# First feed-forward block, larger token group: the input projection by seven block products in halves of 192 tokens

## The chip, the cores and the metric

The kernel runs on one core of one Trainium2 chip. The metric is the device time of one execution in microseconds. Before the change it is 1551.35 us, the median of three runs (1550.58 to 1552.38).

## The reference, cut to what matters

The reference runs one step of a streaming encoder: a convolution layer with a SwiGLU feed-forward block, then a shared key and value projection, an attention layer and a second feed-forward block, for 640 tokens (512 of a prompt, 128 of eight running streams). All of it is in 32-bit floats. The change touches the first feed-forward block:

```python
D_MODEL = 1024
FFN_HIDDEN = -(-8 * D_MODEL // (3 * 256)) * 256        # 2816

def rms_norm(x, g):
    xf = x.astype(jnp.float32)
    y = xf * lax.rsqrt(jnp.mean(xf * xf, axis=-1, keepdims=True) + EPS)
    return (y * g.astype(jnp.float32)).astype(x.dtype)

def swiglu_ffn(h, g, w_in, w_out):
    a, b = jnp.split(rms_norm(h, g) @ w_in, 2, axis=-1)
    return h + (jax.nn.silu(a) * b) @ w_out
```

With 128 rows to a tile, `w_in` has 8 blocks in depth and 22 hidden tiles, each with an `a` half and a `b` half of 128 columns; `w_out` has 22 blocks in depth and 8 output tiles.

## The kernel before

Activations lie with their features on the 128 partitions and the tokens along the row. The residual stream `h` stays on the chip. The tokens are split into a smaller group 0 of 256 and a larger group 1 of 384 tokens (`GR`).

Every 32-bit product is made of three matmuls. A weight tile is loaded as `raw`, rounded by ScalarE to `whi` (fp32r), and the rest `wlo = raw - whi` is formed by VectorE, or by VectorE and GpSimd, which take the share that `pool` names in quarters (`wsplit`, L150 and L154). Activations are split in the same way (`xsplit`, L159 and L160). `mm3` (L170, L171, L172) then adds whi by xhi, wlo by xhi and whi by xlo into one PSUM bank. Each matmul has its own load of a 128x128 weight.

A hidden tile of the feed-forward block is made by `ffn_in`: one weight load of 128x2048 (both halves, 1 MB), two chains of 24 matmuls for each token group, and behind them the gate. `rms_late` leaves the per-token scale out of the activations, so the gate multiplies both halves by it (`bc`, L290 to L293) where the group has such a scale. The hidden tiles of a chunk (4 or 6 of them) are kept, and `ffn_out` multiplies them with the chunk's blocks of `w_out`, adding each output tile to `h` (L303).

The hidden tiles are dealt out as follows. Group 0 does tiles 0 to 17 in three chunks (`FS`) while the convolution of group 1 still runs on VectorE. Then `pw2` of group 1 completes its `h` (L506), and `rms_late` of group 1 (the step "r1" of `PLAN`) makes its activations. Both groups do tiles 18 to 21 together, with each weight split used for both (`FC`). Group 1 then does tiles 0 to 17 alone (`FD`).

The second feed-forward block already makes its input projection in another way, for halves of 320 tokens (`Unit`, L968 in `prod`): the four blocks of the weight (two halves of depth, by `a` and `b`) and the four blocks of the activations (two halves of depth, by two halves of the tokens) are combined by additions so that seven block products, `m1` to `m7`, stand for eight. Some of the additions are made on the weights (L913, VectorE and GpSimd), some on the activations once, and some on the results in PSUM.

The order of instructions on each engine is set by a scheduler that goes by dependencies and by the priorities given in `tc.high_priority`. All weight loads go through one queue (SyncE), into two buffers of `raw`, `whi` and `wlo` each (`wp`). Four PSUM banks (`mm`) and two pairs of banks (`w2`) serve this part.

Of the kernel before, what the change touches and what calls it, by code (L numbers as in the profile page):

```python
# [8 lines left out]
F32 = mybir.dt.float32  # L9
# [33 lines left out]
FD = ((0, 6), (6, 6), (12, 6))  # L43
# [26 lines left out]
PLAN = ("a0 y a1 a2 a4 x a3 a5 a6 l04 p04 l05 d0213 a7 b0 p05 b1 l07 p07 l06 b2 q00 s0 p06 n0 b3 b4 b5 d145 l13 w0 b7 r0 p13 b6 f q16 s1 d101 d127 n1 f f w1 r1")  # L70
# [7 lines left out]
def tile_trunk(ctx, tc, xT, vecs, hist, w_pw1, w_pw2, w_in0, w_out0, w_in1, w_out1,  # L78
# [13 lines left out]
    def nm(s):  # L92
        uid[0] += 1
        return f"{s}_{uid[0]}"
# [176 lines left out]
    def ffn_in(wsrc, j, xs, hid, jj, groups, pool):  # L271
        wh, wl = wsplit(wsrc[j], 16, P, pool=pool)
        for g in groups:
            n = GR[g][1]
            ps = []
            for ab in range(2):
                pt = mmt()
                mm3(pt[:, :n], [(wh[:, (ab * 8 + k) * P:(ab * 8 + k + 1) * P],
                                 wl[:, (ab * 8 + k) * P:(ab * 8 + k + 1) * P]) for k in range(KT)],
                    xk(xs[g], range(KT)))  # L280
                ps.append(pt[:, :n])
# [39 lines left out]
    def ffn(pool, w_in, w_out, xs, groups, chunks, pl=0, og=None, cm=CM, pad=(0, 0)):  # L321
        for j0, ch in chunks:
# [8 lines left out]
            ffn_out(w_out, j0, ch, hid, og or groups, pl)  # L331

# [222 lines left out]
    xs0, xs1 = late[0], late[1]  # L555
# [3 lines left out]
    ffn({0: hp0}, w_in0, w_out0, {0: xs0}, (0,), chunks, PFB)  # L559
# [6 lines left out]
    xs = [rms_late(0, None), rms_late(1, None)]  # L566
# [324 lines left out]
    ENG = {"v": nc.vector, "p": nc.gpsimd}  # L891
    B11, B21, B22, T1, T2, T3, T4 = range(7)
# [18 lines left out]

    def add(e, out, a, b, op=ALU.add):
        ENG[e].tensor_tensor(out=out, in0=a, in1=b, op=op)  # L913

    def copy(out, src):
        nc.scalar.activation(out=out, in_=src, func=AF.Copy)
# [44 lines left out]

    def prod(ps, w, x, first):
        wh, wl = w
        xh, xl = x
        for k in range(4):
            c = slice(k * P, (k + 1) * P)
            for i, (a, b) in enumerate(((wh, xh), (wl, xh), (wh, xl))):
                nc.tensor.matmul(ps, a[:, c], b[:, k, :], start=(first and k == 0 and i == 0),  # L968
                                 stop=(k == 3 and i == 2), skip_group_check=not first)

    def quarter(hi, lo, i):
        return hi[:, 512 * i:512 * i + 512], lo[:, 512 * i:512 * i + 512]

    class Unit:
        def __init__(u, j, hid, jj):
            u.j, u.hid, u.jj = j, hid, jj

        def prep(u, a22=None):
            r = wp.tile([P, 2048], F32, tag="raw", name=nm("raw"))
            nc.sync.dma_start(r, w_in1[u.j])  # L980
            hi = wp.tile([P, 2048], F32R, tag="whi", name=nm("whi"))
            lo = wp.tile([P, 2048], F32R, tag="wlo", name=nm("wlo"))
            if a22 is None:
                bk = wf.tile([P, 2 * 1536], F32R, tag="bk", name=nm("bk"))
                a22 = bk[:, 0:512], bk[:, 1536:2048]
            else:
                bk = None
            q = u.q = [r[:, 512 * i:512 * i + 512] for i in range(4)]
            u.r = r[:, 0:1024]
            with tc.high_priority(offset=HP):  # L990
                xsplit(r[:, 0:1024], hi[:, 0:1024], lo[:, 0:1024])
                xsplit(q[2], *a22)
                add(WE[0], q[0], q[0], q[3], ALU.subtract)
                add(WE[1], q[3], q[3], q[2])
                add(WE[2], q[2], q[2], q[0], ALU.subtract)
                xsplit(r[:, 1024:2048], hi[:, 1024:2048], lo[:, 1024:2048])
                add(WE[3], q[1], q[1], q[2], ALU.subtract)
            u.a11, u.a12, u.s2, u.s1 = [quarter(hi, lo, i) for i in range(4)]
            u.a22 = a22
            if bk is not None:  # L1000
                u.prep_back(bk)

        def prep_back(u, bk=None):
            if bk is None:
                bk = wf.tile([P, 2 * 1536], F32R, tag="bk", name=nm("bk"))
            bh, bl = bk[:, 512:1536], bk[:, 2048:3072]
            with tc.high_priority(offset=HP):
                xsplit(u.r, bh, bl)
            u.s3, u.s4 = [quarter(bh, bl, i) for i in range(2)]

        def m1(u):
            u.pa = bank("pa")[:, 0:HT]
            u.u = tmp("acc")
            prod(u.pa, u.a11, xc[B11], True)
            with tc.high_priority(offset=2 * HP):
                copy(u.u, u.pa)

        def m5(u):
            u.pc = bank("pc")[:, 0:HT]
            u.v = tmp("sq")  # L1020
            prod(u.pc, u.s1, xc[T1], True)
            with tc.high_priority(offset=2 * HP):
                copy(u.v, u.pc)

        def m6(u):
            u.pb = bank("pb")[:, 0:HT]
            prod(u.pb, u.s2, xc[T2], True)
            with tc.high_priority(offset=2 * HP):
                add("v", u.pb, u.pb, u.u)
                add("v", u.pc, u.pb, u.v)  # L1030
# [241 lines left out]
```

## Time and profile before

| what | value |
|---|---|
| median of three runs | 1551.35 us |
| the profiled execution | 1551.3 us |
| its span | 1549.5 us |
| shared tiles 18 to 21 of both groups | about 422 to 506 us of the span |
| group 1 alone, tiles 0 to 17 | about 506 to 732 us |
| second feed-forward block's entry | about 1080 to 1200 us |

In the page, PE is TensorE's matmuls and PEld its weight loads, DVE is VectorE, ACT is ScalarE, POOL is GpSimd. A row of the span in slices gives the busy share in tenths. Matmuls overlap each other, so the length of one says less than the distance from one start to the next; the end of a matmul is modelled. In the order of time, the first column is the start in us from the span's start and the second the length.

### The profile page before, as it was taken

What the parts mean: (1) busy time and instruction counts of PE and PEld (TensorE: products, weight loads), DVE (VectorE), ACT (ScalarE), POOL (GpSimd) and SP (SyncE); (2) the same over time, 40 slices, a digit from 0 to 9 for tenths busy, and PEclk for the clock granted to TensorE, in tenths of its full rate; (3) what the DMA queues carried; (4) which work ended last, traced back from release to release, by engine and by line L of the source; (5) the groups of instructions that cost most, each with busy time, mean ns of one, the idle gap of its engine ahead of it and who ended that gap; (6) DMA issues with size and microseconds to landing.
All of it is one profiled execution on the core that took longest, in us unless ns stands there. A gap on an engine that the chain in (4) does not pass through costs nothing.

```text
span 1549.5 us, 26569 instructions
## 1 busy us (share of the span) xinstructions
PE 1471.7 (95%) x10770; PEld 1398.9 (90%) x10770; DVE 1050.1 (68%) x1863; ACT 662.4 (43%) x1173; POOL 443.8 (29%) x403
## 2 busy tenths in 40 slices
PE   5888998989999999999999999999989999999997
PEld 5878888989999999999988798886989999999997
DVE  6994999988555455457576767566796476476455
ACT  4544454535423323235454445443554244244244
POOL 6865568877501000001321211110411121121110
PEclk9999999999999999999999999998999999999998
DMA  7784434444421333433655545453103213213211
GB/s 236 234 228 142 137 113 159 148 157 153 147 82 55 129 116 129 135 118 126 202 183 201 174 140 205 133 175 114 55 28 109 82 56 109 82 55 109 82 55 68
DMA packets 59658, 199.95 MB, mean 129 GB/s; under 512 B 10128, under 2 KB 22672, under 8 KB 46736
## 3 DMA queue, kind: packets, MB, share of 16 engines
q1 hardware_dynamic: 59248, 197.96, 39.1%
q8 instruction: 84, 1.38, 0.4%
q10 hardware_dynamic: 288, 0.31, 0.1%
q14 instruction: 38, 0.31, 0.1%
HBM read 187.02 MB, written 11.22 MB: 128 GB/s over the span
## 4 chain that ended last, share of the span: by engine, by line
PE 71%; DVE 16%; ACT 3%; issue 3%; DMA 3%; POOL 2%; SPq 0%; POOLq 0%; DVEq 0%; ACTq 0%
PE mm L170 12%; PE mm L172 12%; PE mm L171 12%; PE pb L968 6%; DVE w L437 5%; DVE wlo L154 4%; PE pc L968 4%; PE pa L968 4%; PE pb L170 1%; PE pb L171 1%; PE pb L172 1%; PE pa L172 1%; PE pa L170 1%; PE pc L170 1%; PE pc L172 1%
## 5 line engine op out<-in xcount | busy, mean ns | idle before, releaser
L171 PE MATMUL mm<-x,wlo 128*128 128x256 f32 (+1 forms) x1344 | 416.8, 312 | 15.4 <-DVE wlo L154 14.9
L170 PE MATMUL mm<-x,whi 128*128 128x256 f32 (+1 forms) x1344 | 413.3, 312 | 6.4 <-ACT x L159 3.7
L172 PE MATMUL mm<-x,whi 128*128 128x256 f32 (+1 forms) x1344 | 412.7, 311 | 0.5
L150 ACT ACTIVATE whi<-raw 128x2048 fp32r<-128x2048 f32 (+2 forms) x117 | 197.7, 1694 | 232.6 <-PE mm L172 138.8
L171 PEld LDWEIGHTS mm<-x,wlo 128*128 128x128 f32 x1344 | 257.1, 192 | 18.7 <-DVE wlo L154 17.5
L170 PEld LDWEIGHTS mm<-x,whi 128*128 128x128 f32 x1344 | 254.5, 191 | 11.2 <-ACT x L159 4.1
L172 PEld LDWEIGHTS mm<-x,whi 128*128 128x128 f32 x1344 | 255.1, 191 | 2.9 <-DVE x L160 1.8
L154 DVE TENSOR_TENSOR wlo<-raw,whi 128x2048 fp32r<-128x2048 f32 (+5 forms) x117 | 214.0, 1832 | 62.2 <-ACT whi L150 61.2
L154 POOL TENSOR_TENSOR wlo<-raw,whi 128x1536 fp32r<-128x1536 f32 (+3 forms) x50 | 145.7, 2918 | 69.0 <-ACT whi L150 69.0
L913 POOL TENSOR_TENSOR raw<-raw 128x512 f32<-128x512 f32 x38 | 50.5, 1330 | 332.3 <-DVE raw L913 257.5
L171 PE MATMUL mm<-hid,wlo 128*128 128x256 f32 (+1 forms) x352 | 107.7, 308 | 6.6 <-DVE wlo L154 6.6
L172 PE MATMUL mm<-hid,whi 128*128 128x256 f32 (+1 forms) x352 | 105.8, 307 | 0.2
L170 PE MATMUL mm<-hid,whi 128*128 128x256 f32 (+1 forms) x352 | 104.6, 307 | 0.1
L437 DVE SCALAR_TENSOR_TENSOR w<-gp,dwv,w 128x384 f32<-128x384 f32 x180 | 103.9, 612 | 0.8
L195 POOL TENSOR_TENSOR acc<-sq,sq 128x384 f32<-128x384 f32 (+1 forms) x8 | 8.1, 1006 | 258.2 <-ACT sq L179 258.1
L171 PEld LDWEIGHTS mm<-hid,wlo 128*128 128x128 f32 x352 | 66.0, 188 | 7.8 <-DVE wlo L154 7.8
L417 POOL TENSOR_TENSOR y<-y,cvt 128x256 f32<-128x256 f32 (+1 forms) x60 | 69.3, 1154 | 6.3 <-ACT cvt L416 4.0
L172 PEld LDWEIGHTS mm<-hid,whi 128*128 128x128 f32 x352 | 65.7, 188 | 0.6 <-DVE hid L160 0.6
L159 ACT ACTIVATE whi<-raw 128x1024 fp32r<-128x1024 f32 x38 | 39.4, 1054 | 61.6 <-PE pc L172 18.1
L170 PEld LDWEIGHTS mm<-hid,whi 128*128 128x128 f32 x352 | 65.2, 188 | 0.4 <-ACT hid L159 0.3
L968 PE MATMUL pa<-x0f,whi 128*128 128x320 f32 x228 | 61.2, 316 | 2.5 <-DVE t L913 2.3
L195 POOL TENSOR_TENSOR acc<-acc,sq 128x384 f32<-128x384 f32 (+1 forms) x48 | 52.7, 1097 | 28.9 <-ACT sq L179 27.5
(317 smaller groups left out, 3391.4 us busy)
## 6 DMA issues: line engine op xcount, KB each, us to landing
raw<-in_w_in SPq DMA_DIRECT2D x62, 1024.0 KB
raw<-in_w_out SPq DMA_DIRECT2D x36, 768.0 KB
raw<-in_w_pw SPq DMA_DIRECT2D x22, 1024.0 KB
cache<-in_ck SPq DMA_DIRECT2D x32, 512.0 KB
cache<-in_cv SPq DMA_DIRECT2D x32, 512.0 KB
raw<-in_w_kq SPq DMA_DIRECT2D x8, 1024.0 KB
x<-sc SPq DMA_DIRECT2D x16, 368.0 KB
raw<-in_w_out SPq DMA_DIRECT2D x4, 1024.0 KB
```

The costliest lines, as they stand in the source:

```text
L150: nc.scalar.activation(out=hi[:, a:b], in_=raw[:, a:b], func=AF.Copy)
L154: eng.tensor_tensor(out=lo[:, a:b], in0=raw[:, a:b], in1=hi[:, a:b].bitcast(F32), op=ALU.subtract)
L159: nc.scalar.activation(out=hi, in_=src, func=AF.Copy)
L170: nc.tensor.matmul(ps, wh, xh, start=(i == 0), stop=False)
L171: nc.tensor.matmul(ps, wl, xh, start=False, stop=False)
L172: nc.tensor.matmul(ps, wh, xl, start=False, stop=(i == last))
L195: last["acc"] = eng.tensor_tensor(out=acc[:, :n], in0=prev, in1=s(), op=ALU.add)
L417: nc.gpsimd.tensor_tensor(out=y[g][:, c, :], in0=y[g][:, c, :], in1=pr[:, :n], op=ALU.add)
L437: nc.vector.scalar_tensor_tensor(out=dst, in0=src, scalar=wj, in1=dst, op0=ALU.mult, op1=ALU.add)
L913: ENG[e].tensor_tensor(out=out, in0=a, in1=b, op=op)
L968: nc.tensor.matmul(ps, a[:, c], b[:, k, :], start=(first and k == 0 and i == 0), stop=(k == 3 and i == 2), skip_group_check=not first)
```

## The change

The larger group's part of the first feed-forward block now uses the seven block products too, for all its 22 hidden tiles, in halves of 192 tokens. The code of `Unit` and its helpers moves up and takes a description of the stage (`First` or `Second`: where weights, PSUM, temporaries and results lie).

- `FC` (tiles 18 to 21) runs for group 0 alone, with three quarters of the low part of each weight on GpSimd (`PFB`).
- "r1" leaves the plan. In its place group 1's `h` is scaled by the gain on ScalarE, the row scale is formed as before, and the scaled activations are combined into seven operands of 4 x 192 columns, each split into hi and lo.
- `FD` becomes chunks of 5, 6, 5 and 6 tiles, each tile one `Unit`: `prep` loads 1 MB and makes seven split weight operands of 512 columns, `m1` to `m7` are 12 matmuls of 192 columns each, and PSUM results are added on VectorE between them.
- The eight output tiles of a chunk are dealt out between the units of the next one (`outs1`), each with its own load of `w_out`.
- The host stores the `b` half's two depth halves in swapped order; `ffn_in` reads them so.

```diff
-FD = ((0, 6), (6, 6), (12, 6))
+FD = ((0, 5), (5, 6), (11, 5), (16, 6))
+HQ = 192
+TQ = (slice(0, HQ), slice(HQ, 2 * HQ))
...
-PLAN = ("... n1 f f w1 r1")
+PLAN = ("... n1 f f w1")
...
+    def prod(ps, w, x, first):
+        wh, wl = w
+        xh, xl = x
+        for k in range(4):
+            c = slice(k * P, (k + 1) * P)
+            for i, (a, b) in enumerate(((wh, xh), (wl, xh), (wh, xl))):
+                nc.tensor.matmul(ps, a[:, c], b[:, k, :], start=(first and k == 0 and i == 0),
+                                 stop=(k == 3 and i == 2), skip_group_check=not first)
...
+            with tc.high_priority(offset=HP):
+                xsplit(r[:, 0:1024], hi[:, 0:1024], lo[:, 0:1024])
+                xsplit(q[2], *a22)
+                add(WE[0], q[0], q[0], q[3], ALU.subtract)
+                add(WE[1], q[3], q[3], q[2])
+                add(WE[2], q[2], q[2], q[0], ALU.subtract)
+                xsplit(r[:, 1024:2048], hi[:, 1024:2048], lo[:, 1024:2048])
+                add(WE[3], q[1], q[1], q[2], ALU.subtract)
...
+        def m6(u):
+            u.pb = u.st.pb(u)
+            prod(u.pb, u.s2, u.st.xc[T2], True)
+            with tc.high_priority(offset=2 * HP):
+                add("v", u.pb, u.pb, u.u)
+                add("v", u.pc, u.pb, u.v)
...
+        def m7(u):
+            prod(u.pb, u.s3, u.st.xc[T3], False)
+            with tc.high_priority(offset=2 * HP):
+                u.c = u.st.tmp("acc")
+                add("v", u.c, u.pb, u.v)
...
-    if FC:
-        ffn({0: hp0, 1: hp1}, w_in0, w_out0, {0: xs0, 1: xs1}, (0, 1), FC)
-    ffn({1: hp1}, w_in0, w_out0, {1: xs1}, (1,), FD)
...
+    for k in range(KT):
+        nc.scalar.activation(out=xg[:, k, :], in_=hp(1, k), func=AF.Copy, scale=col(V_NFFN, k))
+    bc, _ = rstd_bc([hp(1, k) for k in range(KT)], 384)
+    bc1 = bca[:, 256:640]
+    nc.scalar.activation(out=bc1, in_=bc, func=AF.Copy)
...
+    for x, i, q in ((b11, B11, 0), (b12, None, 1), (b22, B22, 1), (b21, B21, 0)):
+        add("v", x, x, bc1[:, TQ[q]].unsqueeze(1).to_broadcast([P, 4, HQ]), ALU.mult)
+        if i == B11:
+            put1(i, x)
+    add("v", tq, b12, b11, ALU.subtract)
+    put1(T1, tq)
...
+    ffn({0: hp0}, w_in0, w_out0, {0: late[0]}, (0,), FC, PFB)
...
+    u = unit(0)
+    for f in (u.m1, u.m5, u.m6, u.m2):
+        f()
...
+        if w:
+            w.m1()
+        u.m7()
+        if w:
+            w.m5()
+        u.m3()
+        u.m4()
+        if todo > 1:
+            next(gen, None)
+        if w:
+            w.m6()
+            w.m2()
+        if todo:
+            next(gen, None)
```

What this makes of the engines' order. TensorE, between two hidden tiles of group 1 alone, before (`x` are the activations, two tiles `mm` the `a` and `b` halves of a hidden tile):

```order
L170 MATMUL mm_5287<-x_4424,whi_5282 128x384
L171 MATMUL mm_5287<-x_4424,wlo_5283 128x384
L172 MATMUL mm_5287<-x_4424,whi_5282 128x384
L170 MATMUL mm_5312<-x_4424,whi_5282 128x384
L171 MATMUL mm_5312<-x_4424,wlo_5283 128x384
```

TensorE, in the first chunk of units, after (`x1g` and `xq` hold the activations' operands, `bk` and `whi`, `wlo` the weights'; the `w_620` and `w_632` pairs of banks and the `mm` bank are a unit's pa with pb, and its pc):

```order
L350 MATMUL w_620_5108<-x1g,whi_5093 128x192
L350 MATMUL mm_5137<-x1g,bk_5095 128x192 x9
L350 MATMUL mm_5259<-x1g,whi_5215 128x192
L350 MATMUL mm_5137<-x1g,bk_5095 128x192 x3
L350 MATMUL w_632_5230<-xq,whi_5215 128x192
L350 MATMUL mm_5259<-x1g,wlo_5216 128x192
L350 MATMUL mm_5259<-x1g,whi_5215 128x192 x2
```

In place of chains of 384 columns stand products of 192 columns, and those of two neighbouring units are mixed.

TensorE at the entry, after (`hid` and `mm` are group 0's output tiles of tiles 18 to 21):

```order
L173 MATMUL mm_4834<-hid_4511,wlo_4773 128x256
L174 MATMUL mm_4834<-hid_4511,whi_4772 128x256
L350 MATMUL w_599_4911<-x1g,whi_4896 128x192
L172 MATMUL mm_4848<-hid_4511,whi_4772 128x256
L173 MATMUL mm_4848<-hid_4511,wlo_4773 128x256
```

The first matmul of the first unit stands ahead of the last three output tiles of group 0, which had no such matmul among them.

VectorE at the same place, before, right after `pw2` of group 1 (`n` and `x` are the scaled and the split activations of "r1"):

```order
L154 TENSOR_TENSOR wlo_4622<-raw_4620,whi_4621 128x2048
L160 TENSOR_TENSOR x_4424<-n_539_4425,x_4424 128x384
L160 TENSOR_TENSOR x_4424<-n_540_4429,x_4424 128x384
L255 TENSOR_SCALAR n_541_4433<-h,vec 128x384
L288 TENSOR_TENSOR t_567_4557<-t_566_4556,mm_4531 128x256
```

And after, from the first operation that needs the row scale `bca` (`xg` are the scaled activations, `tq` their combinations, `x1g` and `xq` the split operands):

```order
L339 TENSOR_TENSOR xg_4442<-xg_4442,bca 128x4x192 x4
L339 TENSOR_TENSOR tq_4443<-xg_4442 128x768
L162 TENSOR_TENSOR x1g<-xg_4442,x1g 128x768
L290 TENSOR_TENSOR t_572_4696<-t_571_4695,mm_4670 128x256
L156 TENSOR_TENSOR wlo_4766<-raw_4764,whi_4765 128x512
L339 TENSOR_TENSOR xg_4442<-xg_4442 128x4x192
L162 TENSOR_TENSOR x1g<-xg_4442,x1g 128x768 x2
L162 TENSOR_TENSOR x1g<-tq_4443,x1g 128x768
L162 TENSOR_TENSOR hid_4511<-t_572_4696,hid_4511 128x256
L290 TENSOR_TENSOR t_579_4759<-t_578_4758,mm_4733 128x256
L162 TENSOR_TENSOR xq<-xg_4442,xq 128x768
L339 TENSOR_TENSOR tq_4443<-xg_4442,tq_4443 128x768
```

These operations of 768 elements were not there before, and they stand among group 0's gate products and weight splits. Behind them follow one more weight split of 512, a `hid` split, the a22 split of the first unit, a split of 768, four additions to `h`, a difference of 768, and the split of 1024 that makes the first unit's first weight operands.

More of the change, by code (lines that the diff above doesn't have):

```diff
@@ L554, in tile_trunk @@
         step(tok[0], tok[1:])
-    xs0, xs1 = late[0], late[1]
     cv.close()
@@ new lines, in hid_of, with unit @@
+    def hid_of(c):
+        if c == 1:
+            t = hida
+        elif c % 2:
+            t = hid1a()
+        else:
+            t = cst.tile([P, 2 * KT * 256], F32R, tag="x0", name=nm("hid"))
+        t = t[:, 0:2 * FD[c][1] * 384]
+        return t.rearrange("p (s k n) -> p s k n", s=2, n=384)
+    order = [(j0 + i, c, i) for c, (j0, ch) in enumerate(FD) for i in range(ch)]
+    hids = {}
+    def unit(i):
+        if i >= len(order):
+            return None
+        j, c, jj = order[i]
+        if c not in hids:
+            hids[c] = hid_of(c)
+        u = Unit(First, j, hids[c], jj)
+        u.prep()
+        return u
@@ L960, in plain @@
             gate(ps[0], ps[1], hids[0], jj, c)
[L962 to L972, printed above, removed]
@@ L1146, in tile_trunk @@
         if j + 1 < FT:
-            w = Unit(j + 1, hids[c], where[j + 1][1])
+            w = Unit(Second, j + 1, hids[c], where[j + 1][1])
             w.prep()
```

247 lines of the change are left out of this document (157 added, 90 removed).

## The prediction

> **What bounds the kernel now.** I read the page first (span, busy shares, the 40 slices), then the busy time by stretches around the first feed-forward block, then the order of time on TensorE, because a busy share does not tell how far apart matmuls start.
>
> ```profile
> span 1549.5 us, 26569 instructions
> PE 1471.7 (95%) x10770; PEld 1398.9 (90%) x10770; DVE 1050.1 (68%) x1863; ACT 662.4 (43%) x1173; POOL 443.8 (29%) x403
> PE   5888998989999999999999999999989999999997
> DVE  6994999988555455457576767566796476476455
> ```
>
> TensorE is the bound, and every matmul has a weight load of its own (10770 of each). The profiled execution took 1551.3 us, its span plus 1.8; the median of the three runs is 1551.35, so a sum made against the profile can be read against the median. The stretches (PE, PEld, DVE, ACT, POOL busy with counts, granted clock, DMA share, GB/s):
>
> ```profile
> 204.00:244.00 40.00, 36.22 (x292) 35.14 (x290) 40.00 (x65) 22.48 (x33) 33.89 (x17) 0.96 0.41 122
> ...
> 422.00:506.00 84.00, 84.00 (x591) 84.00 (x590) 43.82 (x69) 28.47 (x48) 8.14 (x9) 1.00 0.22 74
> 506.00:732.00 226.00, 226.00 (x1307) 225.71 (x1305) 119.06 (x146) 78.10 (x96) 7.06 (x6) 1.00 0.37 124
> 732.00:747.00 15.00, 12.43 (x107) 12.35 (x107) 6.55 (x17) 5.27 (x13) 8.40 (x12) 1.00 0.49 162
> 1051.00:1115.00 64.00, 60.81 (x473) 52.14 (x472) 41.17 (x86) 29.89 (x64) 17.07 (x17) 0.92 0.19 64
> 1115.00:1150.00 35.00, 31.26 (x201) 30.50 (x200) 34.36 (x38) 16.79 (x23) 2.59 (x2) 0.95 0.09 31
> ```
>
> From 422 (shared tiles 18 to 21) through 732 (the larger group's other 18 tiles) TensorE never idles, at full clock, with VectorE half busy. So the changed stretch has nothing to win from waits: only fewer or shorter matmuls can shorten it, and any new wait is paid in full. What one matmul costs there is the distance between starts:
>
> ```profile
> 731.34 0.34 PE L170 MATMUL mm<-hid,whi 128*128 128x384 f32 x1
> 731.52 0.34 PE L171 MATMUL mm<-hid,wlo 128*128 128x384 f32 x1
> 731.69 0.34 PE L172 MATMUL mm<-hid,whi 128*128 128x384 f32 x1
> ...
> 734.45 0.28 PE L170 MATMUL mm<-x,whi 128*128 128x256 f32 x1
> 734.56 0.28 PE L171 MATMUL mm<-x,wlo 128*128 128x256 f32 x1
> 734.67 0.28 PE L172 MATMUL mm<-x,whi 128*128 128x256 f32 x1
> ...
> 762.22 0.22 PE L739 MATMUL w<-KK,QQ 128*128 128x128 f32 x1
> 762.28 0.27 PE L740 MATMUL w<-KL,QQ 128*128 128x128 f32 x1
> 762.39 0.33 PE L739 MATMUL w<-KK,QQ 128*128 128x256 f32 x1
> ```
>
> 384 columns take 0.1735 us (two steps make 0.35), 256 take 0.113. No row has 192 columns. The first 128-column matmul gives way after 0.06 us, so streaming alone would put 192 halfway between 0.06 and 0.113: 0.087. But the second gives way only after 0.11. Its successor waits for its weights, as the weight loads at that place show:
>
> ```profile
> 762.22 0.19 PEld L740 LDWEIGHTS w<-KL,QQ 128*128 128x128 f32 x1
> 762.33 0.19 PEld L739 LDWEIGHTS w<-KK,QQ 128*128 128x128 f32 x1
> 762.44 0.19 PEld L740 LDWEIGHTS w<-KL,QQ 128*128 128x128 f32 x1
> ...
> 738.76 0.75 PEld L204 LDWEIGHTS w<-onec,acc 128*128 128x128 f32 x6
> ```
>
> Loads of 128x128 start 0.11 apart, whatever streams beside them; the six of L204 feed matmuls of one column each and still need (0.75 - 0.19) / 5 = 0.112 each. Above 256 columns this floor is hidden behind the stream. At 192 it is not.
>
> **Part 1, seven products for eight.** Before, a hidden tile of the larger group costs 2 x 8 x 3 = 48 matmuls of 384 columns; 22 tiles make 1056 x 0.1735 = 183.2 us. After, it costs 7 x 4 x 3 = 84 of 192 columns, 1848 in all. In columns that is an eighth less (16128 for 18432), but in weight loads 75% more. By the load rows, 1848 x 0.110 = 203.3, **+20.1 us**. The ends for a 192-column matmul: 0.087 by streaming (160.8, -22.4) and 0.113, as it should not exceed one of 256 columns (208.8, +25.6). I take 0.110, since the load rows at 128 columns and at one column agree on it.
>
> The Trainium skill, "TensorE: Matmul & The Clock Gate", section "Back-to-back issue gap", gives about 81 ns a matmul for a sustained stream of load and matmul pairs at 128 columns and 131 at 512; an estimate between them for 192 is 89 ns, which would make 1848 of them 164.5 us, a saving of 18.7. This trace disagrees for its 4-byte operands: pairs at 128 columns are 110 ns apart, and 384 columns take 173.5, so the measurement decides.
>
> Output tiles stay: 22 x 8 x 3 = 528 matmuls of 384 columns before and after.
>
> **Part 2, the way into the products.** Tiles 18 to 21 now run for the smaller group alone: 288 matmuls x 0.1135 = 32.7 us, as many as before, but a new weight is due every 5.4 us where a shared one lasted 13.8. The same step in 204:244 (288 matmuls, x292 in the row) took 39.6 us; what TensorE waited for between 150 and 760 is mostly of this kind (us in total, times, longest):
>
> ```profile
> PE mm L171 <- DVE wlo L154: 21.6, 18, 3.6
> ```
>
> Two points of the order of time around the old row scale, and groups of VectorE by form (after the count: busy us, mean ns of one, then idle time before):
>
> ```profile
> 433.77 0.83 PE L216 MATMUL w<-ident,rt 128*128 128x128 f32 x6
> ...
> 434.64 0.49 ACT L262 ACTIVATE bca<-w 128x384 f32<-128x384 f32 x1 [0.47 <-PE w L216]
> ```
>
> ```profile
> L913 DVE TENSOR_TENSOR xg<-xg,bca 128x1280 f32<-128x1280 f32 x4 | 5.7, 1483 | 0.0
> ...
> L160 DVE TENSOR_TENSOR x0f<-xg,x0f 128x640 fp32r<-128x640 f32 x2 | 1.6, 820 | 0.0
> ...
> L160 DVE TENSOR_TENSOR wlo<-raw,whi 128x1024 fp32r<-128x1024 f32 x25 | 33.2, 1347 | 6.3 <-ACT whi L159 5.8
> L160 DVE TENSOR_TENSOR bk<-raw,bk 128x1024 fp32r<-128x1024 f32 x14 | 22.8, 1630 | 0.1
> L913 DVE TENSOR_TENSOR raw<-raw 128x512 f32<-128x512 f32 x26 | 17.8, 685 | 1.9 <-POOL raw L913 1.8
> ...
> L160 DVE TENSOR_TENSOR bk<-raw,bk 128x512 fp32r<-128x512 f32 x13 | 9.0, 691 | 1.9 <-ACT bk L159 1.7
> ...
> L303 DVE TENSOR_TENSOR h<-mm,h 128x384 f32<-128x384 f32 x32 | 17.5, 554 | 27.8 <-PE mm L172 27.8
> ...
> L303 DVE TENSOR_TENSOR h<-mm,h 128x256 f32<-128x256 f32 x8 | 3.3, 417 | 0.1
> ```
>
> Those 32.7 us must also cover the new preparation. The larger group's row scale needs all of its h, last written as TensorE leaves pw2 at 422.5; the L216 that spreads it ran at 433.8 before, and in the new order stands behind 119 matmuls, so at 436, with the scale copied (0.49) by 436.7. From there VectorE runs, in its own order (the rows shown with the change), 14 operations of 768 elements until the first unit's weights: 0.95 each between the 640 and 1280 rows, 13.3 us; and between them two gate products (0.417) and their splits (0.42), two weight splits of 512 (0.69), one a22 split (0.69), four h additions (0.417) and the first 1024 split (1.35): 6.8. That ends at 456.8, about when TensorE has done this block (422.5 + 32.7 = 455.2). But the first product's matmul stands in TensorE's queue ahead of the block's last three output tiles, and VectorE owes more before both first units have run m1, m5 and m6: a 768 split, four h additions, three 1024 splits, four differences of 512 with GpSimd sums between, an a22 split, two output-weight splits of 640 (0.82) and a 1630 back split, 13.4 us, with some 1.5 of waiting for those output tiles. TensorE ends the six products near 474.5; unhindered it would at 422.5 + 32.7 + 72 x 0.11 = 463.1. **+11 us.** The ends: 4 if the slow tiles above give VectorE time it can use, 16 if the stalls of 204:244 (7 us for the block) add half of themselves. The nearest row is the same entry in the second block, which idles TensorE 3.2 + 3.7 us in 1051:1150 with three plain tiles as its cover. The row-scaled copies that "r1" made (8 scalings, 8 splits on VectorE) go, but TensorE did not wait for them.
>
> **Part 3, the units themselves.** VectorE per unit: two splits of 1024 (2.7), the back split (1.63), a22 (0.69), two differences (1.37), and seven operations of 192 at 0.35 (the line through the 256 and 384 rows): 8.85 us. TensorE: 84 x 0.11 = 9.24. The first five units have no output tiles between them, so VectorE is 96% loaded, and m7, m3 and m4 wait for its additions into PSUM; behind a waiting matmul everything on TensorE waits. From the second chunk each unit has 8/6 output tiles with it: VectorE 8.85 + 8/6 x (0.95 + 0.554) = 10.9, TensorE 9.24 + 8/6 x 18 x 0.1735 = 13.4, which is cover enough. I take 3 us for the first chunk and 2 for the 17 later units, **+5**; ends 1 and 12 (VectorE's 1024 splits all at 1.63, units at 9.4 with queueing). GpSimd's two additions a unit and the 6 MB that are loaded twice hide: DMA is 0.37 busy in 506:732. The end (rms of both groups, 732:747) waits as before: 0.
>
> Sum: 20.1 + 11 + 5 = 36; 1551.3 + 36 = **1587 us**.
>
> **Rivals.** First, the other side: weight loads hide behind the shorter stream, and a matmul costs 0.087. Then part 1 gives -22.4, but a unit's TensorE time falls to 7.3, under VectorE's 8.85, so the first five units cost 5 x 1.5 = 8 more and the entry about 12: 1551, no change; with a covered entry (4) and VectorE at its faster rows, 1537. The deciding point is the spacing: with 16 us of waits the change breaks even at (183.2 - 16) / 1848 = 0.090 us. For it speak the 0.06 of the first 128-column matmul; against it, that this one had its weights in place, and that every following load is 0.11 later.
>
> Second, VectorE bounds the whole stretch: its total is 22 x 8.85 + 32 x 1.5 = 243 us, against 295 for TensorE, so only if every operation stretched by a fifth; then the waits reach 30 and the time is 1603. Third, the entry is worse (TensorE's clock drops in the gaps, as the 0.92 and 0.95 of 1051:1150 show): +25, 1601. Fourth, the entry and the units run almost clean (5 us in all): 1576.
>
> **How the numbers follow.** The forecast with its spread of waits (the fourth case in it) 0.80; the second and third beyond that 0.09; the streaming rival 0.11, of which 0.07 is faster by over 0.2% (3 us, about what a measurement of this kernel can tell from no change) and 0.04 within it. Low end: 0.108 a matmul, as the 0.11 may be rounded (+16.4), and 4 us of waits; high end: 0.113 (+25.6) and 16 + 12 of waits. So 1571 to 1605.
>
> **What would show it.** In the changed trace the 192-column matmuls of a unit start 0.11 apart and their loads too; if 0.087, part 1 is wrong. TensorE idles some 11 us between 440 and 480, released by VectorE; from the second chunk on it is full. The stretch from the end of pw2 to the first attention matmul grows from 309 to about 345 us. The prediction is wrong if loads of 128x128 follow closer than 0.108, or if the waits at the entry are several times 11.

## The result, and the profile after

The changed kernel takes 1602.12 us, the median of four runs (1599.97 to 1605.97); the kernel before took 1550.96 beside it. The ratio is 1.0345, with a 95% interval of 1.0301 to 1.039: slower. The profiled execution took 1599.97 us, with a span of 1598.2, 48.7 more than before's 1549.5. One of the four executions of the kernel with GpSimd's share in four pieces (below) took 2459.82 us at a granted clock of 0.558, where its others had 0.98, and its time below is the median of the other three.

The page of the changed kernel (busy us, share of the span, count; then slices of a fortieth of the span):

```profile
span 1598.2 us, 28734 instructions
PE 1503.2 (94%) x11562; PEld 1425.8 (89%) x11562; DVE 1165.6 (73%) x2062; ACT 735.6 (46%) x1358; POOL 528.6 (33%) x453
PE   5988998889979999999999999999999999999997
PEclk9999999999989999999999999999999999999999
```

TensorE got 792 more matmuls (1848 for 1056). In the 12th slice, 440 to 479 us, PE fell to 7 and the granted clock to 8: that is the way into the products. Order of time on TensorE of the changed kernel (start, length, and in brackets the idle time before and who ended it), at the four points that part the changed stretch:

```profile
419.39 0.28 PE L172 MATMUL mm<-x,whi 128*128 128x256 f32 x1
...
474.30 0.36 PE L350 MATMUL mm<-x1g,wlo 128*128 128x192 f32 x1 [2.61 <-DVE wlo L162]
474.50 0.54 PE L350 MATMUL mm<-x1g,whi 128*128 128x192 f32 x2
...
482.17 0.28 PE L350 MATMUL w<-x1g,whi 128*128 128x192 f32 x1
482.29 0.27 PE L350 MATMUL w<-x1g,wlo 128*128 128x192 f32 x1
...
783.38 0.38 PE L172 MATMUL mm<-x,whi 128*128 128x256 f32 x1 [0.65 <-DVE h L749]
```

The small group's tiles 18 to 21 start at 419.39; the first six products are through at 482.17; the attention's first matmul follows at 783.38. So **the entry** lasts 62.8 us and **the units** 301.2, together 364.0. Before, the same stretch lasted 311.0:

```profile
422.37 0.28 PE L170 MATMUL mm<-x,whi 128*128 128x256 f32 x1
...
733.33 0.36 PE L170 MATMUL mm<-x,whi 128*128 128x256 f32 x1 [1.31 <-DVE h L303]
```

The stretch grew by 53.0; its start came 3.0 earlier and the rest of the program was 1.4 shorter, which leaves 48.7.

Matmuls of 192 columns stand 0.11 apart, as the rows at 482.17 and 482.29 show; the median of the units' is 0.112. That this is the load's floor and not the stream's shows where a unit's matmuls follow an output tile:

```profile
575.14 0.34 PE L172 MATMUL mm<-hid,ohi 128*128 128x384 f32 x1
575.31 0.25 PE L350 MATMUL mm<-x1g,wlo 128*128 128x192 f32 x1
575.40 0.27 PE L350 MATMUL mm<-x1g,whi 128*128 128x192 f32 x1
```

The first matmul of 192 columns had its weights loaded beside the longer stream of 384, and the next one starts 0.087 later, the price of streaming alone that the prediction's first rival used. All 48 of the units' matmuls that stand right behind one of 384 columns give way after 0.085 to 0.092 us; none that follows another of 192 does.

But behind the idle 2.61 us before 474.30 they stand 0.21 apart, until 478.02: half of the clock for 3.7 us (half clock follows the gaps of 3.55 us before 447.21 and of 3.40 before 457.60 as well). The windows of the changed kernel (PE, PEld, DVE, ACT, POOL busy with counts, granted clock, DMA share, GB/s):

```profile
444.00:452.00 8.00, 4.74 (x26) 4.45 (x27) 8.00 (x10) 3.51 (x6) 2.63 (x2) 0.79 0.37 131
452.00:462.00 10.00, 6.01 (x36) 5.53 (x35) 10.00 (x12) 3.65 (x5) 2.92 (x1) 0.78 0.32 105
462.00:472.00 10.00, 8.79 (x64) 8.28 (x63) 7.89 (x12) 5.06 (x8) 3.98 (x2) 0.88 0.21 68
472.00:482.00 10.00, 6.92 (x45) 6.75 (x46) 8.32 (x9) 3.07 (x6) 3.42 (x2) 0.83 0.56 179
...
535.00:759.00 224.00, 222.84 (x1760) 222.27 (x1758) 174.66 (x287) 109.60 (x217) 43.24 (x32) 1.00 0.37 122
```

From 444 to 462 VectorE never rests, and TensorE idles and gets 0.79 and 0.78 of its clock. The longest waits of TensorE from 415 to 790 (total, times, longest) name VectorE:

```profile
PE mm L350 <- DVE wlo L162: 4.1, 3, 2.6
PE mm L172 <- DVE t L290: 3.5, 1, 3.5
PE mm L174 <- DVE hid L162: 3.4, 1, 3.4
```

Each matmul's distance to the next against its distance at full clock (0.1735, 0.1135 and 0.112 by shape) parts the entry's 62.8 us: 42.1 of matmuls, 14.4 in the steps that hold an idle gap (12.5 of it idle) and 6.3 of slow clock in the other steps.

What VectorE did there is in its order of time, of the changed kernel:

```profile
434.63 3.72 DVE L162 TENSOR_TENSOR hid<-t,hid 128x256 fp32r<-128x256 f32 x1
438.27 3.55 DVE L339 TENSOR_TENSOR xg<-xg,bca 128x768 f32<-128x768 f32 x4
...
442.62 4.20 DVE L162 TENSOR_TENSOR x1g<-xg,x1g 128x768 fp32r<-128x768 f32 x1
446.74 0.41 DVE L290 TENSOR_TENSOR t<-t,mm 128x256 f32<-128x256 f32 x1
...
451.15 0.41 DVE L162 TENSOR_TENSOR hid<-t,hid 128x256 fp32r<-128x256 f32 x1
451.49 0.41 DVE L290 TENSOR_TENSOR t<-t,mm 128x256 f32<-128x256 f32 x1
451.82 3.91 DVE L162 TENSOR_TENSOR xq<-xg,xq 128x768 fp32r<-128x768 f32 x1
...
461.13 1.21 DVE L162 TENSOR_TENSOR wlo<-raw,whi 128x1024 fp32r<-128x1024 f32 x1
```

and GpSimd's in the same kernel:

```profile
434.06 4.00 POOL L156 TENSOR_TENSOR wlo<-raw,whi 128x1536 fp32r<-128x1536 f32 x1 [1.66 <-ACT whi L152]
441.99 4.02 POOL L156 TENSOR_TENSOR wlo<-raw,whi 128x1536 fp32r<-128x1536 f32 x1 [3.92 <-ACT whi L152]
451.38 3.54 POOL L156 TENSOR_TENSOR wlo<-raw,whi 128x1536 fp32r<-128x1536 f32 x1 [5.37 <-ACT whi L152]
```

A split of 256 took 3.72 us and one of the same size 0.41; a split of 768 took 4.20 and 3.91, where its like takes 0.95 (below). Each long one starts while GpSimd's 1536 elements run and ends a little after them (434.06 + 4.00 = 438.06 against 434.63 + 3.72 = 438.35). The gate product at 451.49 began beside GpSimd's operation too and took its usual 0.41: it reads one input from PSUM (`mm`), the splits read both from SBUF. TensorE's 3.55 us of idle time end with the gate product of 446.74, which stands behind the split of 4.20.

The Trainium skill, "SBUF — State Buffer", section "Who interferes with whom", says that a VectorE instruction with two SBUF inputs contends with a GpSimd instruction that reads SBUF, as its second input comes through a read interface that the two share, and that the shared pair is an exclusive lock. These rows agree, down to the PSUM reader that is not held; that a split waits for the whole of GpSimd's instruction is what the rows show.

### The profile page after: what moved, and what is told of

Read it like the earlier page. It is cut to its first block, busy times and chain, and to the rows that moved or that the text cites. A ratio compares the mean times of both kernels' runs of the same rounds, so it can differ in the third digit from the quotient of the medians.

```text
span 1598.2 us, 28734 instructions
## 1 busy us (share of the span) xinstructions
PE 1503.2 (94%) x11562; PEld 1425.8 (89%) x11562; DVE 1165.6 (73%) x2062; ACT 735.6 (46%) x1358; POOL 528.6 (33%) x453
## 4 chain that ended last, share of the span: by engine, by line
PE 66%; DVE 19%; DMA 5%; issue 4%; ACT 3%; POOL 2%; SPq 0%; POOLq 0%; DVEq 0%; ACTq 0%
PE mm L172 8%; PE mm L174 8%; PE mm L173 8%; PE w L350 7%; PE pb L350 6%; DVE w L545 5%; PE pc L350 4%; DVE wlo L156 4%; PE pa L350 3%; PE mm L350 3%; PE pb L172 1%; PE pb L173 1%; PE pb L174 1%; PE pa L174 1%; PE w L1038 1%
## 5 line engine op out<-in xcount | busy, mean ns | idle before, releaser
L173 PE MATMUL mm<-x,wlo 128*128 128x256 f32 (+1 forms) x992 | 299.1, 304 | 15.9 <-DVE wlo L156 15.2
L172 PE MATMUL mm<-x,whi 128*128 128x256 f32 (+1 forms) x992 | 295.1, 304 | 5.3 <-ACT x L161 3.7
L339 POOL TENSOR_TENSOR raw<-raw 128x512 f32<-128x512 f32 x82 | 116.1, 1416 | 545.3 <-DVE raw L339 394.0
L174 PE MATMUL mm<-x,whi 128*128 128x256 f32 (+1 forms) x992 | 295.1, 302 | 1.0 <-DVE x L162 0.7
L173 PEld LDWEIGHTS mm<-x,wlo 128*128 128x128 f32 x992 | 190.8, 193 | 19.5 <-DVE wlo L156 18.0
L172 PEld LDWEIGHTS mm<-x,whi 128*128 128x128 f32 x992 | 188.2, 192 | 10.2 <-ACT x L161 4.8
L174 PEld LDWEIGHTS mm<-x,whi 128*128 128x128 f32 x992 | 188.6, 191 | 3.5 <-DVE x L162 2.4
L156 DVE TENSOR_TENSOR wlo<-raw,whi 128x512 fp32r<-128x512 f32 (+5 forms) x87 | 148.7, 1714 | 40.7 <-ACT whi L152 36.6
L162 DVE TENSOR_TENSOR wlo<-raw,whi 128x1024 fp32r<-128x1024 f32 x82 | 106.7, 1315 | 25.2 <-ACT whi L161 22.5
L161 ACT ACTIVATE bk<-raw 128x512 fp32r<-128x512 f32 (+1 forms) x81 | 68.3, 846 | 71.7 <-PE w L350 30.6
L162 DVE TENSOR_TENSOR bk<-raw,bk 128x512 fp32r<-128x512 f32 (+1 forms) x81 | 89.0, 1100 | 6.8 <-ACT bk L161 6.4
L350 PE MATMUL w<-xq,bk 128*128 128x192 f32 x528 | 65.7, 274 | 1.2 <-DVE acc L339 1.2
```

The lines of the kernel that those rows point to most:

```text
L156: eng.tensor_tensor(out=lo[:, a:b], in0=raw[:, a:b], in1=hi[:, a:b].bitcast(F32), op=ALU.subtract)
L161: nc.scalar.activation(out=hi, in_=src, func=AF.Copy)
L162: nc.vector.tensor_tensor(out=lo, in0=src, in1=hi.bitcast(F32), op=ALU.subtract)
L172: nc.tensor.matmul(ps, wh, xh, start=(i == 0), stop=False)
L173: nc.tensor.matmul(ps, wl, xh, start=False, stop=False)
L174: nc.tensor.matmul(ps, wh, xl, start=False, stop=(i == last))
```

## The experiments

Three questions: is the price of the products the load floor; what makes the entry 20 us too long; what holds the units. Times are medians with the ratio to the kernel before in the same job, where that took between 1549.98 and 1555.54; so differences of a few us between two of these kernels are read from the stretches of their traces. "Entry" and "units" are the two stretches above, on the profiled execution.

**Halves of 192 in the kernel before.** Nothing else is changed, so this is part 1 alone, on twice as many matmuls.

```diff
-                mm3(pt[:, :n], [...], xk(xs[g], range(KT)))
+                for c in (slice(0, n // 2), slice(n // 2, n)) if g else (slice(0, n),):
+                    mm3(pt[:, c], [...], [(xs[g][0][:, k, c], xs[g][1][:, k, c]) for k in range(KT)])
```

> The kernel before, with the larger group's two chains of each hidden tile (22 tiles, x 2 halves x 8 blocks x 3) run in two halves of 192 columns: 2112 matmuls of 192 where there were 1056 of 384, and nothing else changed. If each matmul pays for its own weight load (0.112 us, the spacing in the changed kernel), the chains cost 2112 x 0.112 = 236.5 us for 183.2: +53 us, about 1604. If 192 columns cost what streaming says (0.087), 183.7: no change, 1551.

Measured: 1605.37 us, ratio 1.032 (1.0297 to 1.0343). The window of the whole stretch, with TensorE full and its clock at 1.00:

```profile
422.00:760.00 338.00, 338.00 (x2795) 338.00 (x2794) 144.92 (x183) 90.14 (x110) 8.86 (x10) 1.00 0.27 92
```

The 192-column matmuls there are 0.1116 apart in the mean. The load floor holds, and the streaming rival (0.087 for every matmul) falls.

**The products with 128 columns in place of 192.** All but the first matmul of a product move 128 columns, so a third of the results is not computed.

```diff
-                nc.tensor.matmul(ps, a[:, c], b[:, k, :], ...)
+                n = P if ps.shape[1] == HQ and not (first and k == 0 and i == 0) else ps.shape[1]
+                nc.tensor.matmul(ps[:, :n], a[:, c], b[:, k, :n], ...)
```

> The changed kernel, but all matmuls of the first block's products except the first of each starting chain (1782 of 1848) move 128 columns of their 192; the other 64 columns of the products are left out. Weight-load theory: the spacing stays at 0.109 to 0.112, and the time at 1597 to 1602. Streaming theory: a third of the columns goes, 1782 x 0.028 to 0.037 = 50 to 66 us less, 1536 to 1552.

Measured: 1647.2 us, ratio 1.0587 (1.0559 to 1.0615): neither number, but slower than either. The windows show why:

```profile
480.00:535.00 55.00, 55.00 (x258) 54.87 (x258) 24.62 (x41) 15.62 (x30) 7.03 (x6) 0.50 0.21 74
...
660.00:760.00 100.00, 100.00 (x786) 100.00 (x785) 75.44 (x116) 45.70 (x82) 21.22 (x15) 1.00 0.34 112
```

From 480 to 535 TensorE is busy throughout and still gets half its clock. Where the clock is full, most of these matmuls are 0.108 to 0.113 apart, as with 192 columns; at half clock 0.213. So fewer columns save nothing: the floor holds here too, but the time does not test it.

**One operand for all seven products.** The other six operands are not made (13 operations of 768 elements on VectorE and six rounding copies on ScalarE are left out).

```diff
-    for x, i, q in ((b11, B11, 0), (b12, None, 1), (b22, B22, 1), (b21, B21, 0)):
-        ...
+    add("v", b11, b11, bc1[:, TQ[0]].unsqueeze(1).to_broadcast([P, 4, HQ]), ALU.mult)
+    put1(B11, b11)
+    First.xc = [First.xc[B11]] * 7
```

> The changed kernel, but all seven products use one activation operand (the first): 3 scalings, 4 differences and 6 splits of 768 elements are left out on VectorE, 12.4 us at 0.95, and the 6 splits on ScalarE. Matmuls are unchanged. Theory that VectorE's queue sets the entry: 12 to 20 us less, 1582 to 1590, more than 12 if the drop of TensorE's clock in the gaps goes too. Theory that the row scale or the weights set it: within 3 us of 1602.

Measured: 1590.71 us, ratio 1.0227 (1.0192 to 1.0262). Entry 51.7 instead of 62.8, units 301.5. The operands' work in VectorE's queue is worth 11 us of the entry.

**The weights of the first two units kept.** From the third unit on, no weights are prepared; the first two units' are used.

```diff
-        u.prep()
+        if i < 2:
+            u.prep()
+            made.append(u)
+        else:
+            v = made[i % 2]
+            u.a11, u.a12, u.s2, u.s1, u.a22 = v.a11, v.a12, v.s2, v.s1, v.a22
+            u.s3, u.s4 = v.s3, v.s4
```

> The changed kernel, but from the third unit on the split weights of the first two are used again: 20 MB of loads and 20 preparations on ScalarE, VectorE and GpSimd are left out; matmuls are unchanged. Theory that weight preparation holds the units back: the waits after 482 us of the span (10 us in all, some 7 of them not at the end) go, 1593 to 1596. Theory that the matmul spacing alone sets the units: within 3 us of 1602.

Measured: 1592.38 us, ratio 1.0247 (1.0216 to 1.0279). Entry 62.4, units 295.9: the preparation holds the units up by 5.3 us. The stretch starts 2.2 later and the program behind it is 3.9 shorter than in the changed kernel, so the time itself tells less than the stretch does.

**Plain chains in the changed stages.** The split stages stay; the products and their operands go, and the step "r1" is back in the plan.

```diff
-        if w:
-            w.m1()
-        u.m7()
-        ...
+        ffn_in(w_in0, j, {1: late[1]}, {1: (hids[c][:, 0], hids[c][:, 1])}, jj, (1,), 0)
```

> The changed kernel with its split stages kept (the first four output rows for the small group alone, chunks of 5, 6, 5 and 6 for the larger group, output tiles dealt between its steps), but each unit of the larger group is two plain chains of 24 matmuls of 384 columns again, and the seven operands are not made. The part of theory that puts all of the loss on the products, on their operands and on the waits of their units (24 + 22 + 8 less 3 that the earlier stages gained): about the time before, 1548 to 1556. The rival, that splitting the first four rows by group and dealing the tiles costs time by itself (the four rows' weights are prepared twice, once per group, 22 rows of weights instead of 18 after the split): 1560 to 1575.

Measured: 1563.42 us, ratio 1.0097 (1.0073 to 1.0121). **The rival's time came true**: the split stages cost 13 us without any product, and the theory that the products, their operands and their waits make up all of the loss fell. The reason that the rival gave, weights prepared twice, is not shown by this; the plain chains without GpSimd's share, below, test it.

**GpSimd's share taken away.** All low parts of the four rows on VectorE, first in the changed kernel:

```diff
-    ffn({0: hp0}, w_in0, w_out0, {0: late[0]}, (0,), FC, PFB)
+    ffn({0: hp0}, w_in0, w_out0, {0: late[0]}, (0,), FC, 0)
```

> The changed kernel with all low parts of the small group's four rows on VectorE, none on GpSimd (before the change of place three quarters of each were GpSimd's, 1536 elements a piece). VectorE gets 12 x 1.85 us for 1536 elements each = 22 us more of own work in about 50 us, 6 of these (11 us) between the end of the pointwise stage and the first product. Theory A, the queue alone: the entry grows by about 8 to 11 us, 1610 to 1613. Theory B, GpSimd's operations hold VectorE up: the three held operations (3.72, 4.20 and 3.91 us instead of 0.41, 0.94 and 0.94) give back 9.5 us against the 11 of new work, so 1600 to 1606.

Measured: 1592.48 us, ratio 1.0273 (1.0247 to 1.0299): faster than the changed kernel, and than theory B's own numbers. Groups of VectorE from 419 to 482 (count, then busy us, mean ns of one, idle before), of the changed kernel:

```profile
L156 DVE TENSOR_TENSOR wlo<-raw,whi 128x512 fp32r<-128x512 f32 x5 | 10.1, 2022 | 4.0 <-ACT whi L152 2.9 <-POOL acc L197 1.1
L162 DVE TENSOR_TENSOR x1g<-xg,x1g 128x768 fp32r<-128x768 f32 x3 | 6.0, 2031 | 0.0
...
L162 DVE TENSOR_TENSOR hid<-t,hid 128x256 fp32r<-128x256 f32 x4 | 5.0, 1240 | 0.0
L162 DVE TENSOR_TENSOR xq<-xg,xq 128x768 fp32r<-128x768 f32 x1 | 3.9, 3912 | 0.0
```

and of this one:

```profile
L156 DVE TENSOR_TENSOR wlo<-raw,whi 128x2048 fp32r<-128x2048 f32 x5 | 11.4, 2287 | 2.4 <-ACT whi L152 2.4
...
L162 DVE TENSOR_TENSOR x1g<-xg,x1g 128x768 fp32r<-128x768 f32 x3 | 2.8, 949 | 0.0
...
L162 DVE TENSOR_TENSOR hid<-t,hid 128x256 fp32r<-128x256 f32 x4 | 1.7, 418 | 0.0
...
L162 DVE TENSOR_TENSOR xq<-xg,xq 128x768 fp32r<-128x768 f32 x1 | 0.9, 950 | 0.0
```

VectorE does four times the elements of `wlo` and needs only 1.3 us more for them; the other three groups give back 3.2, 3.3 and 3.0. Against the 0.69 of a 512 split that is not held, GpSimd's share saved VectorE 5 x (2.287 - 0.69) = 8.0 us and cost it 5 x (2.022 - 0.69) + 9.5 = 16.2. My expectation counted three held operations and left out the weight splits, two of which were held themselves (4.04 and 4.02 us at 421.60 and 427.04; the other three took 0.68 or 0.69). The entry is 53.8 instead of 62.8, the units 301.7.

**The operands' low parts on GpSimd,** the opposite edit, for T1 to T4:

```diff
-        xsplit(src, *First.xc[i])
+        if i < T1:
+            xsplit(src, *First.xc[i])
+            return
+        hi, lo = First.xc[i]
+        nc.scalar.activation(out=hi, in_=src, func=AF.Copy)
+        nc.gpsimd.tensor_tensor(out=lo, in0=src, in1=hi.bitcast(F32), op=ALU.subtract)
```

> The changed kernel with the low parts of the four combined operands T1 to T4 (4 x 768 elements, 0.95 us each on VectorE) made by GpSimd, where 1536 elements took 3.6 us, so about 1.9 us each. Theory A, VectorE's queue is simply too long at the entry: 4 x 0.95 = 3.8 us less in it, the six first products end 3 to 4 us earlier, 1598 where the changed kernel has 1602. Theory B, a two-input VectorE operation that starts beside a two-input GpSimd operation ends only with that: the four GpSimd operations hold VectorE up for as long as they run, up to 4 x 1.9 = 7.6 us, against 3.8 saved, so 1602 to 1606, and in the trace VectorE operations beside them that take 2 us instead of 0.4 to 0.9.

Measured: 1607.15 us, ratio 1.0373 (1.0352 to 1.0395), entry 66.0. Less work in VectorE's queue did not make it sooner: the entry is 3.2 longer, as theory B expects, though the interval of the ratio overlaps the changed kernel's. The queue's length alone (1598) does not explain it. One difference of 768, for example, now falls beside GpSimd's next weight split:

```profile
456.72 3.91 DVE L339 TENSOR_TENSOR tq<-xg,tq 128x768 f32<-128x768 f32 x1
```

**GpSimd's share in four pieces of 384.**

```diff
-                for eng, a, b in ((nc.vector, a, c), (nc.gpsimd, c, b)):
+                parts4 = [(nc.gpsimd, c + (b - c) * q // 4, c + (b - c) * (q + 1) // 4) for q in range(4)]
+                for eng, a, b in [(nc.vector, a, c)] + (parts4 if four else [(nc.gpsimd, c, b)]):
```

> The changed kernel with each GpSimd operation of 1536 elements in the small group's four rows cut into four of 384, the same elements on the same engines. Theory A, the queue alone: GpSimd's fixed cost per operation makes its parts later, if anything; 1602 to 1606. Theory B, a VectorE operation of two inputs that starts beside a GpSimd one waits for the end of that one instruction: the waits shrink from up to 3.7 us to about 1 us, the three held operations give back about 6 to 9 us, and the six first products end that much earlier: 1593 to 1598. If the hold goes on for as long as GpSimd has instructions queued, the long operations stay as they are, and the time too.

Measured: 1600.01 us, ratio 1.0337 (1.031 to 1.0365), entry 61.0. That lies between the ranges of both theories: the long holds are gone, but only 1.8 us of the entry are won. VectorE's order of time in this kernel, and GpSimd's:

```profile
433.69 1.22 DVE L165 TENSOR_TENSOR hid<-t,hid 128x256 fp32r<-128x256 f32 x1
...
448.10 1.75 DVE L342 TENSOR_TENSOR xg<-xg 128x768 f32<-128x768 f32 x1
```

```profile
439.36 6.57 POOL L159 TENSOR_TENSOR wlo<-raw,whi 128x384 fp32r<-128x384 f32 x4 [0.19 <-ACT whi L154]
```

Each held operation now waits about 0.8 us for one piece (1.22 for 0.41, 1.75 for 0.95), and more of them do. GpSimd is held in its turn: the four pieces take 6.57 us together, and the operation of 1536 elements at the same place took 4.02. So the hold is by the instruction, and its sum need not shrink with the pieces.

**Plain chains, GpSimd's share taken away** (the two edits above together):

> The kernel of plain chains of 384 in the changed stages (it took 1563 where the kernel before took 1550), with all low parts of the small group's four rows on VectorE. In that kernel TensorE idles 10.7 us between 387 and 473, and its granted clock is 0.92 and 0.94 there. If GpSimd's operations hold VectorE up and that is what the split of the four rows by group costs: 1550 to 1556. If the cost is that a new row of weights is due every 5.4 us, for VectorE's queue as well: 1563 to 1572.

Measured: 1555.98 us, ratio 1.0033 (1.002 to 1.0045). Waits of TensorE from 385 to 735, first with GpSimd's share:

```profile
PE mm L173 <- DVE wlo L156: 7.0, 3, 4.0
PE mm L174 <- DVE hid L162: 2.8, 1, 2.8
```

and without it:

```profile
PE mm L173 <- DVE wlo L156: 4.9, 2, 4.0
```

The wait for the split of a hidden tile is gone, and from the small group's first matmul to the larger group's first of 384 columns there is 0.2 us of idle time where there were 6.5. What stays is one wait of 4.0 us within pw2, before the entry, that both plain kernels have and the changed kernel has not. So the split by group costs nothing by its weights being due every 5.4 us, as long as VectorE is not held and has no operands to make; of the plain kernel's 13.4 us over the kernel before, 4.6 are left.

**What is left.** One operand, kept weights and no GpSimd share, all at once (six operands, and the weights of all units but two, are left out):

> The changed kernel with three things at once: one operand for all seven products (the other six and their scalings are left out), the weights of the first two units used again by the later ones, and all low parts of the small group's four rows on VectorE. Nothing but the matmuls should be left of the loss: 1848 at 0.1122 against 1056 at 0.1735 is 24 us, with 2 to 8 us at the entry and the end, so 1576 to 1582. If the products' additions into PSUM hold TensorE back by themselves, 1585 or more.

Measured: 1578.15 us, ratio 1.0182 (1.0163 to 1.0201). Entry 44.5, units 296.0. The windows:

```profile
535.00:735.00 200.00, 200.00 (x1594) 200.00 (x1592) 76.21 (x178) 57.25 (x144) 1.00 (x1) 1.00 0.17 49
```

TensorE is full at full clock, and the kernel is still slower than before by 27 us. The stretch is 340.5 us where it was 311.0 before, and 24.1 of these 29.5 are the products' own price by their spacing.

**The kernel before without GpSimd's share** in the small group's first 18 rows, a try for a kernel that beats both:

```diff
-PFA = 3
-PFB = 3
+PFA = 0
+PFB = 0
```

> The kernel before, with all low parts of the small group's first 18 rows on VectorE too (three quarters of each were GpSimd's). VectorE's busy time was 148.7 of 150 us between 150 and 300 and 18 operations of 512 elements took 1.94 us there in the mean, where those that start alone take 0.69, and 18 splits of 256 took 1.56 instead of 0.41: 22.5 + 20.7 = 43 us of holding, against 18 x 1.6 = 29 us of new own work. If GpSimd's operations hold VectorE up: some of 14 us is gained, 1538 to 1548. If VectorE's queue counts alone: 1560 to 1575.

Measured: 1571.41 us, ratio 1.0132 (1.0112 to 1.0153): a loss, in the range that the queue's theory gave, but not by VectorE. Its waits from 150 to 440:

```profile
PE w L204 <- POOL acc L195: 13.4, 2, 12.3
PE mm L171 <- DVE wlo L154: 11.6, 10, 2.5
```

The splits of 256 fall to 0.46 us in the mean and the wait for `wlo`, 21.6 before, to 11.6, as the hold says. But one wait of 12.3 us for GpSimd's sum for a row mean takes its place, before pw2 of the larger group. Why that sum came later in the new order was not tried; no version here beats the kernel before.

## Why the prediction came out as it did

The sign and the range (1571 to 1605) hold, the time of 1587 is 15 short, and the range held it only near its upper end; the stretch, forecast at about 345 us, lasts 364.0. That it held is in part luck: part 2 came out beyond its own end, part 3 stayed under its end, and the program outside the stretch became 4.4 us shorter, for which the prediction had no term. The time lies between those of the third rival (1601, a worse entry through the clock) and the second (1603); the third is nearer to what happened, though the clock is 6.3 of the entry's 22. Two sums of the rivals do not close by the terms that they name (30 us of waits give 1601 and not 1603, the streaming rival's 8 and 12 give 1549 and not 1551); nothing hangs on them. By its steps:

**TensorE is the bound, any wait is paid in full.** Right: the stretch's 53.0 us are 24.1 of matmuls and the rest in waits and clock.

**Part 1, +20.1.** Mechanism right, size slightly off. The spacing is 0.1122 and not 0.110, so 1848 x 0.1122 = 207.3 against 183.2: +24.1. The load rows had given 0.11 to two digits and 0.112 from the six of L204; I took the lower. The kernel in which little else is left is 27 slower than before. The estimate of 89 ns between the figures of the Trainium skill, "TensorE: Matmul & The Clock Gate", section "Back-to-back issue gap", does not hold for these operands: the median here is 112. The Trainium skill, the same page, section "LDWEIGHTS (loading the stationary operand)", gives 1/1.2 ns for each column, an estimate of 107 for these loads, and the 0.108 to 0.114 of the matmuls here lie close to it.

**Part 2, +11.** This step failed in size: 62.8 us for the 40.8 that 288 and 72 matmuls take (32.7 + 8.1) is +22, twice the forecast and beyond its own end of 16. On TensorE the 22 are 14.4 in steps with an idle gap, 6.3 of slow clock and 1.3 of the row scale's small matmuls, which the stretch of before had too. The idle time itself came near the sign that the prediction gave (some 11 us; the windows from 444 to 482 lack 11.5); the slow clock it had only as a rival.

On VectorE, which sets when the products can start, the times counted from the start of the stretch show where it went wrong. The first operation that needs the row scale was due after 14.3 us (436.7 less 422.4) and came after 18.9, behind the hidden split of 3.72. From there to the end of the first 1024 split 20.1 were forecast and 24.1 passed, 6.2 of them the holds of two splits of 768. From there to the end of the six products 17.7 were forecast and 19.8 passed. So the prices failed: splits of 256 at 0.42 and operands at 0.95 are rows of VectorE alone (the two weight splits behind the row scale did take their 0.69). In the changed kernel GpSimd makes three quarters of these weights' low parts in that very stretch, which it had not for the shared rows of before (their low parts were VectorE's alone). Where it did so before, in group 0's 18 tiles, the trace of before had the price (groups of VectorE from 150 to 425):

```profile
L154 DVE TENSOR_TENSOR wlo<-raw,whi 128x512 fp32r<-128x512 f32 x18 | 34.9, 1939 | 3.0 <-ACT whi L150 3.0
L160 DVE TENSOR_TENSOR hid<-t,hid 128x256 fp32r<-128x256 f32 x18 | 28.2, 1564 | 0.0
```

Taking the share away gives 9.0 us of the entry, leaving out operands 11.1; both, with the later units' weights kept as well, give 18.3, and then 44.5 are left, with 2.1 in steps with a gap. And one reason that the prediction gave is refuted: that a weight is due every 5.4 us costs nothing when VectorE is not held, as the plain kernel shows.

**Part 3, +5.** Right in kind. The other 1776 matmuls of the products at 0.1122 and 528 of the output tiles at 0.1735 take 290.9 us, the units took 301.2: 10.3 over. Without weight preparation 5.3 of it go. Of the other 5, the trace of that run has 2.2 in three gaps at the stretch's end (0.94 and 0.60 for ScalarE's rounding of output weights, 0.65 for an addition to `h`), where the prediction had no more than before, which idled 1.31 there; the rest was not parted further. The three parts close: 24.1 + 22.0 + 10.3, less the 3.5 by which the 311.0 of before exceeded its own matmuls (32.7 + 183.2 + 91.6), is 52.9 of the 53.0.

**The rival with VectorE as the bound of the whole stretch** is out: it is busy 174.66 of 224 us from 535 to 759, and TensorE 222.84.

## What to carry to other kernels

What a block product scheme saves in columns it loses in weight loads where a matmul's stream is shorter than its load: seven products of 192 columns cost 84 x 0.112 = 9.4 us here for 48 x 0.1735 = 8.3. Before handing part of a two-input SBUF operation to GpSimd, add to VectorE's side all the two-input operations that will start beside it, each held until GpSimd's instruction ends; here 1536 elements saved VectorE 1.6 us and cost it 3.2. The three gaps of 2.6 to 3.6 us at the changed kernel's entry were paid twice, once as the gap and once as 3 to 7 us of half clock behind it. How short a gap may be was not tried: without GpSimd's share gaps of 1.1 and 1.2 us (at 454.59 and 465.60) had half clock behind them too, and one of 1.2 in the changed kernel's units (at 494.29) had not.

## What the hardware showed that was not expected

GpSimd's hold of VectorE, as above: up to 4.20 us for an operation of 0.95, by whole instructions, and not for an operation with an operand in PSUM. GpSimd is held as well: pieces of 384 elements that take 1.0 us alone take up to 1.7 beside VectorE's.

TensorE's clock stayed at one half for over 100 us although TensorE was never idle in them. In the kernel that moves 128 columns, these windows come behind the one from 480 to 535 shown above:

```profile
535.00:575.00 40.00, 40.00 (x189) 40.00 (x189) 18.60 (x28) 14.00 (x25) 6.37 (x5) 0.50 0.16 53
...
580.00:585.00 5.00, 5.00 (x21) 5.00 (x21) 1.07 (x3) 0.70 (x2) 0.00 (x0) 0.50 0.00 0
585.00:600.00 15.00, 15.00 (x121) 15.00 (x121) 10.92 (x19) 6.89 (x12) 2.57 (x2) 1.00 0.37 115
```

The clock fell at an idle gap of 2.6 us before 476.5, as at the same gap of the changed kernel, where it was back after 3.7 us. Here, with shorter streams between the same loads, it came back only at 585, within a row of output tiles of 384 columns. That a load-bound stream of 128 columns counts as too little activity fits, but is only argued: no run varied the columns further. The Trainium skill, "TensorE: Matmul & The Clock Gate", section "What's actually happening", has the full clock return after at least one busy window of about 3.4 us. The changed kernel's 3.7 agrees; this kernel's 105 or so would be some thirty such windows.
